# Paced gather requests and fixed-order heads in a two-layer streaming encoder

## The chip, the cores and the metric

The kernel runs on one core of one Trainium2 chip. The metric is the device time of one execution in microseconds. The core's engines are PE (matmul), DVE (vector), ACT (scalar), POOL (GpSimd, which here also issues the gathers) and SP (which issues the weight loads); each runs its own instructions in order and waits for the others by semaphores. Sixteen DMA engines move all data.

## What is computed

One inference step of a two-layer encoder for 384 tokens of width 1024: one prompt of 256 frames and eight streams of 16 further frames. Layer 0 mixes with a Mamba-2 scan, layer 1 with sliding-window attention; each is followed by a PEER layer, in which every token picks 128 of 16384 experts by product keys:

```python
def peer(xn, w_q, sub_k1, sub_k2, u_tab, v_tab):
...
        q = (xb @ w_q).reshape(PEER_TOKEN_BLOCK, PEER_HEADS, PEER_QDIM)
        s1 = jnp.einsum('thd,nd->thn', q[..., :PEER_HALF], sub_k1)
        s2 = jnp.einsum('thd,nd->thn', q[..., PEER_HALF:], sub_k2)
        v1, i1 = lax.top_k(s1, PEER_TOPK)
        v2, i2 = lax.top_k(s2, PEER_TOPK)
...
        gate = jax.nn.softmax(vs.astype(jnp.float32), axis=-1).reshape(PEER_TOKEN_BLOCK, PEER_HEADS * PEER_TOPK)
        ue = jnp.take(u_tab, eid, axis=0)
        act = jax.nn.gelu(jnp.einsum('tkd,td->tk', ue, xb).astype(jnp.float32))
        ve = jnp.take(v_tab, eid, axis=0)
        return jnp.einsum('tk,tkd->td', (gate * act).astype(xb.dtype), ve)
...
            h = h + mix
            h = h + peer(rmsnorm(h, norm_ffn[l]), p_w_q[l], p_sub_k1[l], p_sub_k2[l], p_u[l], p_v[l])
        y = rmsnorm(h, norm_final)
```

## The kernel before

The 384 tokens are three blocks of 128: blocks 0 and 1 are the prompt (256 tokens), block 2 holds the streams. h lies in SBUF as [128, 3, 1024]. Matmuls in full precision are made of three passes: `split` cuts a tile into hi (ACT, L130 or L133) and lo (DVE, L131 or L134), and `gemm_cols` and `gemm_rows` multiply hi·hi, hi·lo and lo·hi.

The program runs in one line: Mamba mixer (to 384 us of the profiled span), `peer(0)` (to about 1320), the shared key and value projection and attention (to about 1475), `peer(1)` (to 2412), `final`.

A PEER layer treats its two groups of tokens differently. For the **prompt** it multiplies with all experts: pass 1 has 128 steps, one for each row of 128 experts, of u products (L166 to L168), pass 2 has 128 steps of v products (L179). I number the steps 0 to 127 and 128 to 255. From step 64 on the order of PE, DVE and ACT is held to the order in which the code is written (`in_order`); POOL and SP are ordered by a scheduler, which places an instruction by its readiness in a simulated execution. For the **streams** (block 2) it gathers only the rows that are picked, 128 x 1024 floats (512 KB) per gather, all issued by POOL in one queue (L1232):
- a *u row* (`fetch_u`) goes into one of three or four buffers `gath`, and DVE multiplies it with the tokens (L1279, `u_item`). `U_DUE` says how many are done by which step, and each is asked for two or three items ahead.
- four *v rows* make a *quad* (`fetch_v`, `v_quad`): sixteen matmuls with the coefficients `cm` (L1349). `V_DUE` says at which step a quad stands. A row needs a *place*, four slots of the big array G, from the list `V_SLOTS`, and `taken` notes which are in use; a place is free again as soon as its quad is written.
- an *item* (`fetch_item`, `v_item`) is a v row that DVE adds up itself (L1304), from step `I_DUE[0]` on.

`tick` and `quads` are called once per step and write these requests down.

At the head of `peer` each block of h gets the mixer's result (`add`: L653 in layer 0, L919 in layer 1), is squared on ACT (L971), its mean goes to the power −1/2 on POOL (L976), it is scaled on DVE (L979) and transposed on PE (L988), and the query products follow. The tile qTp takes both the squares' output and the scaled rows. h then goes to DRAM (`spill`) and comes back near the end of pass 2 (L1591), where the PEER result is added (L1597). The attention head and `final` repeat that norm through `rstd_of` (L200 to L204) and `normed_T` (L223, L227).

Of the kernel before, what the change touches and what calls it, by code (L numbers as in the profile page):

```python
# [19 lines left out]
P = 128  # L20
# [46 lines left out]
def encoder_step(ctx: ExitStack, tc: tile.TileContext, t_in, t_out):  # L67
# [102 lines left out]
    def gemm_rows(accs, terms, first, last):  # L170


        for b, halves in enumerate(accs):
            n = halves[0].shape[-1]
            for i, ((whi, wlo), xhi, xlo) in enumerate(terms):
                st, sp = first and i == 0, last and i == len(terms) - 1
                for x, w, s_, e_ in ((xhi(b), whi, st, False), (xhi(b), wlo, False, False), (xlo(b), whi, False, sp)):
                    for hf, ps in enumerate(halves):
                        mm = pe.matmul(ps, x, w[:, hf * n:(hf + 1) * n], start=s_, stop=e_)  # L179
                        if len(terms) > 1:  # L180
                            pin(mm)
# [10 lines left out]
    def rstd_of(h, order=range(NB)):  # L192

        ss = T(small, [P, NB], F32, tag="ss")
        s2 = T(small, [P, NB, 2], F32, tag="ss2")
        r = T(small, [P, NB], F32, tag="rstd")
        for b in order:
            c = slice(b, b + 1)
            for hf in range(2):
                sq = act.activation(bank([P, 512]), h[:, b, hf * 512:hf * 512 + 512], AF.Square,  # L200
                                    accum_out=s2[:, b, hf:hf + 1])
            dve.tensor_tensor(ss[:, c], s2[:, b, 0:1], s2[:, b, 1:2], op=OP.add)
            dve.tensor_scalar(ss[:, c], ss[:, c], 1.0 / D, EPS, op0=OP.mult, op1=OP.add)
            pool.tensor_tensor(r[:, c], ss[:, c], mhalf[:, c], op=OP.pow)  # L204
        after["act"] = sq
        return r

    after = {}

    @contextmanager  # L210
    def behind():

        with ExitStack() as c:
            for i in after.values():
                c.enter_context(tc.issue_after(i.ins))
            yield

    def normed_T(pls, xn, h, r, gis, use, order):

        outs = [(T(pl, [P, KD, NT], F32R, tag=f"xhi{i}"), T(pl, [P, KD, NT], F32R, tag=f"xlo{i}"))  # L220
                for i, pl in enumerate(pls)]
        for b in order:
            after["dve"] = dve.tensor_scalar(xn[:, b], h[:, b], r[:, b:b + 1], None, op0=OP.mult)  # L223
        for k in range(KD):
            ps = bank([P, NT])
            for b in order:
                pe.transpose(ps[:, b * P:(b + 1) * P], xn[:, b, k * P:(k + 1) * P], ident)  # L227
            for (hi, lo), gi in zip(outs, gis):
                split(hi[:, k], lo[:, k], ps, scale=gcol[:, gi, k:k + 1])
            use(k, outs)  # L230
        return outs
# [18 lines left out]
    def mamba(h_src):  # L250
        with ExitStack() as c:
# [17 lines left out]
            with tc.tile_pool(name="mxn", bufs=1) as xn_pool:  # L269
                xn = T(xn_pool, [P, NB, D], F32, tag="xn")  # L270
                r = rstd_of(h)
                for b in range(NB):
                    dve.tensor_scalar(xn[:, b], h[:, b], r[:, b:b + 1], None, op0=OP.mult)
# [48 lines left out]
            if True:  # L322
# [327 lines left out]
                def add(b):  # L650
# [7 lines left out]
    def attention():  # L658
        with ExitStack() as c:
# [41 lines left out]
            for s in range(NSEQ):  # L701
                pool.memset(maskS[:, s, P + s * TS:P + (s + 1) * TS], 0.0)
# [1008 lines left out]
```

## Time and profile before

| | us |
|---|---|
| median of 3 runs | 2423.77 (2420.09 to 2424.36) |
| the profiled execution | 2425.08 |
| its span | 2423.4 |
| PE busy | 2321.5 |
| DVE busy | 1964.2 |
| ACT busy | 1250.2 |
| POOL busy | 768.1 |

The profile shows one execution. A row of the timeline has the start and length in us, the engine, the line of the kernel, the operation, what it writes and reads, how many, and in brackets how long the engine stood idle before it and what released it. The queue `q1` carries the loads of SP and `q0` those of POOL; here are their packets, their bytes, and the time of their packets as a share of the span of all sixteen DMA engines:

```profile
q1 hardware_dynamic: 99936, 365.85, 41.7%
q0 software_dynamic: 76928, 281.07, 31.1%
```

Most of q0 is gathers: 256 u rows, 192 v rows and 64 items for the two layers, 512 KB each.

### The profile page before, as it was taken

What the parts mean: (1) busy time and instruction counts of PE and PEld (TensorE: products, weight loads), DVE (VectorE), ACT (ScalarE), POOL (GpSimd) and SP (SyncE); (2) the same over time, 40 slices, a digit from 0 to 9 for tenths busy, and PEclk for the clock granted to TensorE, in tenths of its full rate; (3) what the DMA queues carried; (4) which work ended last, traced back from release to release, by engine and by line L of the source; (5) the groups of instructions that cost most, each with busy time, mean ns of one, the idle gap of its engine ahead of it and who ended that gap; (6) DMA issues with size and microseconds to landing.
All of it is one profiled execution on the core that took longest, in us unless ns stands there. A gap on an engine that the chain in (4) does not pass through costs nothing.

```text
span 2423.4 us, 44427 instructions
## 1 busy us (share of the span) xinstructions
PE 2321.5 (96%) x16591; PEld 1991.9 (82%) x16592; DVE 1964.2 (81%) x4233; ACT 1250.2 (52%) x2428; POOL 768.1 (32%) x779
## 2 busy tenths in 40 slices
PE   8899999999998999999998998999998999998997
PEld 7899988999997997666776777999997897666675
DVE  5988846979987899887776675979987899887776
ACT  5656524434565676563343554344475666554343
POOL 2222200011244334555562100012244434556561
PEclk9999999999999999999999999999999999999999
DMA  5555434457798889999995415366798889999995
GB/s 203 175 187 179 154 136 160 137 203 243 261 334 309 319 310 328 399 389 388 369 417 169 149 62 171 123 219 238 257 333 313 307 307 332 399 392 378 384 407 187
DMA packets 177080, 649.76 MB, mean 268 GB/s; under 512 B 21136, under 2 KB 23040, under 8 KB 174208
## 3 DMA queue, kind: packets, MB, share of 16 engines
q1 hardware_dynamic: 99936, 365.85, 41.7%
q0 software_dynamic: 76928, 281.07, 31.1%
q8 instruction: 130, 2.13, 0.4%
q14 instruction: 86, 0.70, 0.1%
HBM read 630.62 MB, written 18.06 MB: 268 GB/s over the span
## 4 chain that ended last, share of the span: by engine, by line
PE 79%; DVE 9%; DMA 4%; issue 3%; ACT 2%; another core or an unknown queue 1%; POOL 1%; SPq 0%; POOLq 0%; DVEq 0%; ACTq 0%
PE bank L179 26%; PE bank L166 11%; PE bank L168 11%; PE bank L167 11%; PE bank L1349 4%; PE bank L1437 3%; DVE lo L131 3%; DMA gath<-in_p_u,eidU 3%; PE bank L1404 2%; PE bank L1362 2%; ACT hi L130 1%; DVE gath L1279 1%; PE bank L533 1%; PE bank L472 1%
## 5 line engine op out<-in xcount | busy, mean ns | idle before, releaser
L130 ACT CAST hi<-raw 128x1024 fp32r<-128x1024 f32 (+1 forms) x476 | 495.8, 1042 | 686.5 <-PE bank L167 318.8
L131 DVE TENSOR_TENSOR lo<-raw,hi 128x1024 fp32r<-128x1024 f32 (+1 forms) x476 | 576.4, 1211 | 172.1 <-ACT hi L130 153.5
L1232 POOL DMA_INDIRECT gath<-in_p_u,eidU x226 | 279.7, 1238 | 779.3 <-DVE gath L1279 443.0
L168 PE MATMUL bank<-xhi,lo 128*128 128x256 f32 (+1 forms) x1344 | 397.0, 295 | 24.1 <-DVE lo L131 22.8
L166 PE MATMUL bank<-xhi,hi 128*128 128x256 f32 (+1 forms) x1344 | 403.5, 300 | 0.5 <-issue 0.4
L167 PE MATMUL bank<-xlo,hi 128*128 128x256 f32 (+1 forms) x1344 | 393.9, 293 | 0.0
L1232 POOL DMA_INDIRECT G<-in_p_v,eidT x192 | 236.7, 1233 | 155.6 <-PE bank L1349 98.4
L168 PEld LDWEIGHTS bank<-xhi,lo 128*128 128x128 f32 x1344 | 255.3, 190 | 29.5 <-DVE lo L131 27.3
L166 PEld LDWEIGHTS bank<-xhi,hi 128*128 128x128 f32 x1344 | 255.7, 190 | 15.6 <-issue 7.8
L167 PEld LDWEIGHTS bank<-xlo,hi 128*128 128x128 f32 x1344 | 255.6, 190 | 0.5
L166 PE MATMUL bank<-qhi,hi 128*128 128x256 f32 (+1 forms) x784 | 232.8, 297 | 0.0
L168 PE MATMUL bank<-qhi,lo 128*128 128x256 f32 (+1 forms) x784 | 227.5, 290 | 2.4 <-DVE lo L131 2.4
L167 PE MATMUL bank<-qlo,hi 128*128 128x256 f32 (+1 forms) x784 | 228.4, 291 | 0.0
L130 ACT CAST hix<-raw 128x1024 fp32r<-128x1024 f32 x118 | 123.9, 1050 | 194.7 <-PE bank L179 85.5
L179 PE MATMUL bank<-hi,phi 128*128 128x512 f32 x632 | 204.3, 404 | 0.2
L1392 ACT ACTIVATE oa<-ioh,e2T 128x128 f16<-128x128 f16 x512 | 163.4, 390 | 79.7 <-PE bank L1404 67.2
L179 PE MATMUL bank<-lo,phi 128*128 128x512 f32 x632 | 197.0, 393 | 6.8 <-DVE lo L131 6.8
L179 PE MATMUL bank<-hi,plo 128*128 128x512 f32 x632 | 195.5, 391 | 0.0
L131 DVE TENSOR_TENSOR lox<-raw,hix 128x1024 fp32r<-128x1024 f32 x118 | 143.9, 1219 | 29.3 <-ACT hix L130 25.1
L1279 DVE SCALAR_TENSOR_TENSOR gath<-gath,G 128x1024 f32<-128x1024 f32 x112 | 136.4, 1219 | 37.2 <-DMA gath<-in_p_u,eidU 37.2
L168 PEld LDWEIGHTS bank<-qhi,lo 128*128 128x128 f32 x784 | 148.1, 189 | 2.8 <-DVE lo L131 2.8
L167 PEld LDWEIGHTS bank<-qlo,hi 128*128 128x128 f32 x784 | 148.8, 190 | 0.4
(396 smaller groups left out, 5155.0 us busy)
## 6 DMA issues: line engine op xcount, KB each, us to landing
raw<-in_u_t SPq DMA_DIRECT2D x256, 512.0 KB
raw<-in_p_v SPq DMA_DIRECT2D x256, 512.0 KB
raw<-in_w_in SPq DMA_DIRECT2D x32, 512.0 KB
raw<-in_p_w_q SPq DMA_DIRECT2D x32, 512.0 KB
raw<-in_w_z SPq DMA_DIRECT2D x16, 512.0 KB
s<-in_state_ssm SPq DMA_DIRECT2D x8, 1024.0 KB
out_sm_ssm<-s SPq DMA_DIRECT2D x8, 1024.0 KB
raw<-in_w_out SPq DMA_DIRECT2D x16, 512.0 KB
```

The source lines that it names most:

```text
L130: act.copy(hi, raw)
L131: dve.tensor_tensor(lo, raw, hi32, op=OP.subtract)
L166: pe.matmul(ps, whi[:, s], xhi[:, k, c0:c1], start=(k == 0), stop=False)
L167: pe.matmul(ps, whi[:, s], xlo[:, k, c0:c1], start=False, stop=False)
L168: pe.matmul(ps, wlo[:, s], xhi[:, k, c0:c1], start=False, stop=(k == KD - 1))
L179: mm = pe.matmul(ps, x, w[:, hf * n:(hf + 1) * n], start=s_, stop=e_)
L1232: pool.indirect_dma_start(out=tile_, out_offset=None, in_=tab, in_offset=bass.IndirectOffsetOnAxis(ap=idx, axis=0))
L1279: pin(dve.scalar_tensor_tensor(tile_, tile_, 1.0, xg[g], op0=OP.mult, op1=OP.mult, accum_out=au[g][:, j:j + 1]))
L1349: pe.matmul(out_s[hf][32 * q:32 * q + 32, :], cm[:, q], rows[q][:, hf * 512:hf * 512 + 512], start=(r == 0), stop=False, tile_position=(0, ...
L1362: pe.matmul(ps, wt[0][:, k * P:(k + 1) * P], xf[:, k], start=(k == 0), stop=(k == KD - 1))
L1392: act.activation(a[:, i], ioh, AF.Square, scale=-1.0, bias=e2T[:, t, 0:1])
L1437: pe.matmul(accs[b][hf], G[e2 // HE][:, e2 % HE, b * P:(b + 1) * P], wt[0][:, hf * 512:hf * 512 + 512], start=False, stop=False)
```

## The change

Requests: `room` grows by `PACE`, 1.6, with each step, up to 1.6; every gather takes one off, and a v row or an item is only asked for while `room` is not negative. A place counts as free two steps after its quad. `V_DUE`, `V_SLOTS`, `U_DUE` and `I_DUE` have new numbers.

Heads: the class `Norm` takes the place of `rstd_of`; the mean is one DVE instruction, the factor 1/1024 goes into the square. At the head of `peer`, at the end of pass 2, at the head of attention and in `final` the adds, squares, powers and scales of the three blocks stand interleaved in a fixed order; qTp and sk move into a pool of their own at lower addresses; the masks of attention are written after the norms' powers; the transposes at the attention head are written several times over. `gemm_rows` runs its last call one half of a bank after the other. The spill is three DMAs.

```diff
-I_DUE = (203, 250)
+I_DUE = (206, 250)
+PACE = 1.6
-U_DUE = ((64, 22), (128, 68), (192, 115), (203, P))
-V_DUE = ([82, 86, 90, 94, 98, 103] + [149 + 6 * i for i in range(10)] + [207 + 11 * (i // 2) for i in range(8)])
-V_SLOTS = [(1, 36 + 4 * i, 66, 100 + 4 * i) for i in range(6)] + [(0, e, 128 + e + 5, 256) for e in (0, 4, 8, 12, 20, 24, 28, 32)]
+U_DUE = ((64, 22), (128, 68), (192, 115), (206, P))
+V_DUE = [82, 85, 90, 95, 102, 148, 156, 162, 167, 171, 177, 181, 186, 192, 197, 203,
+         213, 218, 223, 228, 233, 237, 243, 247]
+V_SLOTS = [(1, e, 66, 64 + e) for e in range(28, 60, 4)] + [(0, e, 128 + e + 5, 256) for e in (0, 4, 8, 12, 20, 24, 28, 32, 56, 60)] + [(0, 16, 209, 256)]
...
+            m = len(halves)
+            for part in ([[hf] for hf in range(m)] if last else [range(m)]):
+                for i, ((whi, wlo), xhi, xlo) in enumerate(terms):
...
+                        for hf in part:
+                            mm = pe.matmul(halves[hf], x, w[:, hf * n:(hf + 1) * n], start=s_, stop=e_)
...
+    class Norm:
...
+        def rstd(self, b):
             c = slice(b, b + 1)
+            dve.scalar_tensor_tensor(self.ss[:, c], self.s2[:, b, 0:1], EPS, self.s2[:, b, 1:2], op0=OP.add, op1=OP.add)
+            self.last = pool.tensor_tensor(self.r[:, c], self.ss[:, c], mhalf[:, c], op=OP.pow)
...
+            with in_order():
+                nrm.scale(2, xn[:, 2])
+                nrm.rstd(0)
+                ends(1, 0)
...
+                ends(1, 1)
+                nrm.scale(0, xn[:, 0])
+                nrm.rstd(1)
...
+                nrm.scale(1, xn[:, 1], 2)
+                for b, n in ((2, 3), (0, 2), (1, 1)):
+                    for _ in range(n):
+                        turn(range(5), [b])
...
+            with tc.issue_after(nrm.last.ins):
+                masked()
+                constants()
...
+            qp0 = tc.tile_pool(name="pq0", bufs=1)
...
+            qTp = T(qpool0, [P, 2 * PH, NP], F32, tag="qTp")
...
-                for b in range(NB):
-                    add(b)
-                    squares(b)
-                    normed(b, 1 + (b == 2))
...
+                sums(0, 0)
+                sums(0, 1)
+                sums(1, 0)
+                nrm.rstd(0)
+                nrm.scale(0, xn[0])
+                sums(1, 1)
+                sums(2, 0)
+                nrm.rstd(1)
+                sums(2, 1)
+                nrm.scale(1, xn[1])
+                nrm.rstd(2)
+                nrm.scale(2, xn[2], 2)
...
-                taken.add(slot)
+                taken[slot] = 2 * NKEY + HE
+                room[0] -= 1
...
-                    taken.discard(slot)
+                    taken[slot] = s + 2
...
+            def ends(b, hf):
+                hh = h[:, b, hf * 512:hf * 512 + 512]
+                dve.tensor_tensor(hh, hh, (accs[b] if b < 2 else out_s)[hf], op=OP.add)
+                nrm.square(b, hf)
...
+                room[0] = min(room[0] + PACE, PACE)
...
-                if s % 4 == 3 and s < V_DUE[0]:
-                    return
-                if done["f"] < (first if s < 2 * HE else 4 * len(QR)) and v_slot(done["f"], s):
+                if (done["f"] < (first if s < 2 * HE else 4 * len(QR)) and room[0] >= 0 and v_slot(done["f"], s)):
...
+                if e2 == 2 * HE - 2:
+                    ends(2, 0)
+                    ends(2, 1)
+                    nrm.rstd(2)
+            ends(0, 0)
+            ends(0, 1)
...
+                out(2, 0, D)
+                nrm.rstd(0)
+                ends(1, 0)
+                ends(1, 1)
+                out(0, 0, 512)
+                nrm.rstd(1)
+                out(0, 512, D)
+                out(1, 0, 512)
+                out(1, 512, D)
```

Three places show how the instructions move. First POOL in pass 2 of layer 0, where the last u rows are gathered (`gath` and `gathx` are u rows; `G<-in_p_v,eidT` are v rows and `G<-in_p_v,eidU` items; x4 is four such rows in turn). Before:

```order
L1232 DMA G_626_3975<-in_p_v,eidT_3971 128x1024 x4
L1232 DMA gath_13237<-in_p_u,eidU_3964 128x1024
L1232 DMA gathx_13263<-in_p_u,eidU_3964 128x1024
L1232 DMA gath_13289<-in_p_u,eidU_3964 128x1024
L1232 DMA gath_13314<-in_p_u,eidU_3964 128x1024
L1232 DMA gath_13341<-in_p_u,eidU_3964 128x1024
L1232 DMA gathx_13375<-in_p_u,eidU_3964 128x1024
L1232 DMA G_626_3975<-in_p_v,eidT_3971 128x1024 x3
```

and now:

```order
L1250 DMA G_626_3972<-in_p_v,eidT_3968 128x1024 x4
L1250 DMA gath_13083<-in_p_u,eidU_3961 128x1024
L1250 DMA gathx_13149<-in_p_u,eidU_3961 128x1024
L1250 DMA gath_13175<-in_p_u,eidU_3961 128x1024
L1250 DMA gath_13203<-in_p_u,eidU_3961 128x1024
L1250 DMA G_626_3972<-in_p_v,eidT_3968 128x1024 x3
L1250 DMA gath_13259<-in_p_u,eidU_3961 128x1024
L1250 DMA G_626_3972<-in_p_v,eidT_3968 128x1024
```

Six u rows between two quads have become four; the four v rows of a quad still stand together.

Second, DVE at the end of pass 2 of layer 0, where h (`h_14759`, now `h_14762`) gets its sums: the first two of these rows write block 2 and wait for h from DRAM; lo and plo belong to the last v tiles. Before:

```order
L1597 TENSOR_TENSOR h_14759<-h_14759,bank_7480 128x512
L1597 TENSOR_TENSOR h_14759<-h_14759,bank_7481 128x512
L131 TENSOR_TENSOR lo_14765<-raw_14762,hi_14764 128x1024
L131 TENSOR_TENSOR plo_14769<-G_1210_7475,phi_14768 128x256
L202 TENSOR_TENSOR ss_14920<-ss_2551_14921 128x1
L203 TENSOR_SCALAR ss_14920<-ss_14920 128x1
L131 TENSOR_TENSOR lo_14787<-raw_14784,hi_14786 128x1024
```

and now:

```order
L133 TENSOR_TENSOR lo_14815<-raw_14812,hi_14814 128x1024
L133 TENSOR_TENSOR plo_14819<-G_1210_7478,phi_14818 128x256
L133 TENSOR_TENSOR lo_14837<-raw_14834,hi_14836 128x1024
L133 TENSOR_TENSOR plo_14841<-G_1210_7478,phi_14840 128x256
L1468 TENSOR_TENSOR h_14762<-h_14762,bank_7483 128x512
L1468 TENSOR_TENSOR h_14762<-h_14762,bank_7484 128x512
L210 SCALAR_TENSOR_TENSOR ss_14765<-ss_2511_14766 128x1
```

The sums of block 2 have moved behind the last lo.

Third, ACT at the head of `peer(1)`, with what the rows wait for: casts of the last weight tile of attention and of the first one of the queries, and between them the six squares into qTp. Before:

```order
L130 CAST hi_16463<-raw_16461 128x1024 [waits DMAHW3_49,DVE_49,PE_49]
L130 CAST hix_16543<-raw_16536 128x1024 [waits DMAHW4_49]
L971 ACTIVATE qTp_16531,ss_2856_16541<-h_14759 128x512 [waits DVE_49,PE_49]
L971 ACTIVATE qTp_16531,ss_2856_16541<-h_14759 128x512 [waits DVE_49] x5
L1021 CAST hi_16603<-raw_16538 128x1024 [waits DMAHW5_49,Activation_49]
```

and now:

```order
L132 CAST hi_16485<-raw_16483 128x1024 [waits DMAHW6_49,DVE_49,PE_49]
L132 CAST hix_16571<-raw_16563 128x1024 [waits DMAHW7_49]
L205 ACTIVATE qTp_16554,ss_2856_16568<-h_14762 128x512 [waits DMASW4_49,DMASW3_49,DMASW5_49,DMASW2_49,DMASW6_49,DMASW1_49,DMASW7_49,DMASW0_49,DVE_49]
L205 ACTIVATE qTp_16554,ss_2856_16568<-h_14762 128x512 [waits DVE_49] x5
L1038 CAST hi_16632<-raw_16565 128x1024 [waits DMAHW0_49,PE_49,Activation_49]
```

The first square waits for transfers of POOL's queue and DVE where it waited for PE.

More of the change, by code (lines that the diff above doesn't have):

```diff
@@ L174, in gemm_rows @@
             n = halves[0].shape[-1]
[L175 to L181, printed above, removed]
+            m = len(halves)
+            for part in ([[hf] for hf in range(m)] if last else [range(m)]):
+                for i, ((whi, wlo), xhi, xlo) in enumerate(terms):
+                    st, sp = first and i == 0, last and i == len(terms) - 1
+                    for x, w, s_, e_ in ((xhi(b), whi, st, False), (xhi(b), wlo, False, False), (xlo(b), whi, False, sp)):
+                        for hf in part:
+                            mm = pe.matmul(halves[hf], x, w[:, hf * n:(hf + 1) * n], start=s_, stop=e_)
+                            if len(terms) > 1:
+                                pin(mm)
     def gemm_row_loop(accs, terms):
@@ L190, in gemm_row_loop @@
                 held, n = [], n + 1
[L192 to L197, printed above, removed]
-            c = slice(b, b + 1)
[L199 to L231, printed above, removed]
+    class Norm:
+        def __init__(self, h):
+            self.h = h
+            self.ss = T(small, [P, NB], F32, tag="ss")
+            self.s2 = T(small, [P, NB, 2], F32, tag="ss2")
+            self.r = T(small, [P, NB], F32, tag="rstd")
+        def square(self, b, hf, out=None):
+            act.activation(bank([P, 512]) if out is None else out, self.h[:, b, hf * 512:hf * 512 + 512], AF.Square,
+                           scale=1.0 / 32, accum_out=self.s2[:, b, hf:hf + 1])
+        def rstd(self, b):
+            c = slice(b, b + 1)
+            dve.scalar_tensor_tensor(self.ss[:, c], self.s2[:, b, 0:1], EPS, self.s2[:, b, 1:2], op0=OP.add, op1=OP.add)
+            self.last = pool.tensor_tensor(self.r[:, c], self.ss[:, c], mhalf[:, c], op=OP.pow)
+        def scale(self, b, out, parts=1):
+            for i in range(parts):
+                w = slice(i * D // parts, (i + 1) * D // parts)
+                dve.tensor_scalar(out[:, w], self.h[:, b, w], self.r[:, b:b + 1], None, op0=OP.mult)
@@ L270, in mamba @@
                 xn = T(xn_pool, [P, NB, D], F32, tag="xn")
-                r = rstd_of(h)
+                nrm = Norm(h)
                 for b in range(NB):
-                    dve.tensor_scalar(xn[:, b], h[:, b], r[:, b:b + 1], None, op0=OP.mult)
+                    nrm.square(b, 0)
+                    nrm.square(b, 1)
+                    nrm.rstd(b)
+                for b in range(NB):
+                    nrm.scale(b, xn[:, b])
                 split(wdh, wdl, wdt)
@@ L728, in attention, with turn @@
-            (khi, klo), (qhi, qlo) = normed_T((kpool, xpool), xn, h, r, (4, 1), kv_block, DONE)
+            ends, nrm = hold.pop("end")
+            khi, klo = [T(kpool, [P, KD, NT], F32R, tag="xhi0"), T(kpool, [P, KD, NT], F32R, tag="xlo0")]
+            qhi, qlo = [T(xpool, [P, KD, NT], F32R, tag="xhi1"), T(xpool, [P, KD, NT], F32R, tag="xlo1")]
+            kw = {0: load_raw(t_in["w_kv"][0:P, :], 512)}
+            turned = {}
+            def turn(ks, bs):
+                for k in ks:
+                    if k not in turned:
+                        turned[k] = bank([P, NT])
+                    for b in bs:
+                        pe.transpose(turned[k][:, b * P:(b + 1) * P], xn[:, b, k * P:(k + 1) * P], ident)
@@ L963, in peer, with sums @@
             raws = [load_raw(t_in["p_w_q"][l, ct]) for ct in range(2)]
[L964 to L979 removed]
+            nrm = Norm(h)
+            def sums(b, hf):
+                add(b, hf)
+                nrm.square(b, hf, xn[b][:, hf * 512:hf * 512 + 512])
             turned = {}
@@ L1251, in v_slot @@
             def v_slot(n, s):
-                return next((k for *k, s0, s1 in V_SLOTS if s0 <= s and V_DUE[n // 4] <= s1 and tuple(k) not in taken), None)
-            taken = set()
+                return next((k for *k, s0, s1 in V_SLOTS if s0 <= s and V_DUE[n // 4] <= s1 and taken.get(tuple(k), 0) <= s), None)
+            taken = {}
+            room = [0.0]
             due = []
@@ L1460, in tick @@
                     fetch_u(done["u"] + 2 + ("u" in more))
+                    room[0] -= 1
                     u_item(done["u"])
```

134 lines of the change are left out of this document (64 added, 70 removed).

## The prediction, written before the changed kernel had run

> **What bounds the kernel now.** I read the page's busy table first, then windows of the stages and of 20 us, then the chain of work that ended last and the timeline of each engine at the places where PE, the TensorE matmul engine, stands still.
>
> ```profile
> PE 2321.5 (96%) x16591; PEld 1991.9 (82%) x16592; DVE 1964.2 (81%) x4233; ACT 1250.2 (52%) x2428; POOL 768.1 (32%) x779
> ```
>
> PE is busy 2321.5 of 2423.4 us, so a microsecond is gained only where PE is idle or runs at a lower clock. The change takes no matmul away (it adds 31 transposes), so some 102 us are to be shared out. The windows say where the gaps of the two passes lie (columns: window, then for PE, PEld, DVE, ACT, POOL the busy us, then the granted clock, the DMA share and GB/s).
>
> ```profile
> 655.00:893.00 238.00, 227.72 (x2260) 213.57 (x2259) 203.63 (x313) 152.96 (x310) 95.65 (x82) 0.99 0.88 317
> 893.00:1297.00 404.00, 396.20 (x2207) 284.31 (x2205) 337.66 (x522) 204.22 (x377) 205.79 (x164) 0.99 0.96 371
> 740.00:760.00 20.00, 14.65 (x115) 12.84 (x116) 12.44 (x21) 8.47 (x18) 6.57 (x7) 0.88 0.87 322
> 1080.00:1100.00 20.00, 20.00 (x129) 13.60 (x129) 17.87 (x31) 10.41 (x21) 11.58 (x9) 1.00 0.99 390
> 1120.00:1140.00 20.00, 15.20 (x64) 9.85 (x63) 13.29 (x22) 5.30 (x8) 9.87 (x8) 0.83 0.93 351
> ```
>
> The first row is the second half of pass 1 of layer 0, the second its pass 2: PE idles 10.3 and 7.8 us there, and a mean clock of 0.99 costs 1% more, 2.4 and 4 us, so about 12 us can be won in each of the four passes. In 740–760 PE loses 5.4 us, in 1120–1140 4.8 us, and the clock falls as well. In 1080–1100, with the DMA engines just as full (0.99, 390 GB/s), PE loses nothing. So a full DMA alone does not stop PE. The same pairs of dips come again in layer 1, some 1092 us later.
>
> All terms below are against the profiled execution, 2425.08 us (span 2423.4 and 1.7 around it). The median of the runs shown is 2423.77, 1.3 lower; I take that off at the end.
>
> **The change, part by part: requests in pass 2.** What stops PE near 1124 us:
>
> ```profile
> 1107.48 1.74 POOL L1232 DMA_INDIRECT G<-in_p_v,eidT  x1 [1.56 <-PE bank L1349]
> 1113.68 1.55 POOL L1232 DMA_INDIRECT gath<-in_p_u,eidU  x1 [0.30 <-issue]
> 1119.30 0.94 POOL L1232 DMA_INDIRECT gath<-in_p_u,eidU  x1 [0.30 <-issue]
> 1113.68 11.94 DMA gath<-in_p_u,eidU
> 1125.65 1.23 DVE L1279 SCALAR_TENSOR_TENSOR gath<-gath,G 128x1024 f32<-128x1024 f32 x1 [7.13 <-DMA gath<-in_p_u,eidU]
> 1128.61 3.64 PE L1349 MATMUL bank<-G,cm 128*32 128x512 f32 x16 [4.80 <-DVE cm L1336]
> ```
>
> POOL waits for the quad's matmuls (L1349) to release the places, then sends four v rows back to back from 1107.48 on and four u rows behind them. The u row sent at 1113.68 takes 11.94 us to land; DVE stands 7.13 us on it, the quad's coefficients (cm) stand behind that product in DVE's fixed order, and PE waits 4.80 us. Three or four u rows are in flight at once. Between steps 192 and 203 the old table asks for 13 u rows in 11 steps; at some 3.2 us a step that is one in 2.7 us, and three in flight cover 8 us, less than 11.94. The new table asks for 13 in 14 steps, one in 3.4 us, so three cover 10 and four 13.6 us. Counted by the planner's rules, all requests there fall from 9 in four steps to 6.
>
> But the order of POOL's instructions shows that the four v rows still stand together and are followed by four u rows, since they still wait for the same matmuls of PE. So the wait shrinks and does not go: I take **a little under half of the 12, −5.5 us per layer, −11 for both**. Ends: 0, and −12 per layer.
>
> **Requests in pass 1.** The two stalls of layer 0:
>
> ```profile
> 730.05 0.96 POOL L1232 DMA_INDIRECT G<-in_p_v,eidT  x1 [0.72 <-PE bank L1349]
> 748.12 0.94 POOL L1232 DMA_INDIRECT G<-in_p_v,eidT  x1 [6.90 <-PE bank L1349]
> 756.09 0.69 DVE L1410 SCALAR_TENSOR_TENSOR G<-bank,G 128x512 f32<-128x512 f32 x1 [6.70 <-remote]
> 757.97 0.38 PE L168 MATMUL bank<-xhi,lo 128*128 128x256 f32 x1 [3.54 <-DVE lo L131]
> ```
>
> Each time POOL has just waited for a quad (0.72 and 6.90 us) and issues five or six gathers in 7 us; DVE then waits 6.70 us for an answer from PE, and PE 3.54 us for the lo that stands behind. After the change POOL's order has eight v rows at the start instead of six, then again three u rows, four v rows, two u rows and four v rows (before: three and one around a u row). The stretch that stalls is the same; only what follows is thinner. I take **−1 us per layer, −2**; ends +3 per layer (the longer first burst, and the second quad due one step sooner, priced at the 3.54) and −12.
>
> **Heads and tails.** Head of peer(0), first three DVE rows, then PE:
>
> ```profile
> 382.53 1.40 DVE L653 SCALAR_TENSOR_TENSOR h<-bank,rs,h 128x512 f32<-128x512 f32 x2
> 386.21 1.41 DVE L653 SCALAR_TENSOR_TENSOR h<-bank,rs,h 128x512 f32<-128x512 f32 x2
> 389.21 0.88 DVE L979 TENSOR_SCALAR qTp<-h,rstd 128x512 f32<-128x512 f32 x2 [0.65 <-POOL rstd L976]
> 386.44 1.28 PE L988 MATMUL bank<-ident,qTp 128*128 128x128 f32 x10 [1.80 <-DVE qTp L979]
> 389.76 1.50 PE L988 MATMUL bank<-ident,qTp 128*128 128x128 f32 x6 [2.03 <-DVE qTp L979]
> 390.00:393.00 3.00, 3.00 (x13) 2.87 (x13) 1.24 (x3) 1.57 (x4) 0.00 (x0) 0.50 0.62 262
> ```
>
> Block after block, DVE adds two halves (1.41), waits for ACT's squares and POOL's power, and scales: 3.68 us from add to add. In the new order the adds of the next block fill those waits. DVE's own work is six halves (4.2), three scales (2.4) and three sums (0.5), 7.1 us where 11.3 were taken; but the last block's add, squares, power and scale stay one behind the other. PE's waits here are 1.80 and 2.03 us. I take **−2** (ends 0 and −5.5: both waits, and 1.7 for the stretch at a clock of 0.50).
>
> Head of peer(1), ACT, then DVE, then PE:
>
> ```profile
> 1475.04 0.63 ACT L971 ACTIVATE qTp<-h 128x512 f32<-128x512 f32 x1 [7.04 <-PE bank L179]
> 1469.36 1.28 DVE L919 TENSOR_TENSOR h<-h,bank 128x512 f32<-128x512 f32 x2
> 1484.39 0.88 DVE L979 TENSOR_SCALAR qTp<-h,rstd 128x512 f32<-128x512 f32 x2 [0.65 <-POOL rstd L976]
> 1478.15 0.41 PE L988 MATMUL bank<-ident,qTp 128*128 128x128 f32 x2 [3.15 <-DVE qTp L979]
> 1481.72 2.37 PE L988 MATMUL bank<-ident,qTp 128*128 128x128 f32 x10 [3.16 <-DVE qTp L979]
> 1479.00:1486.00 7.00, 3.44 (x15) 3.07 (x16) 3.34 (x8) 4.74 (x12) 1.09 (x2) 0.50 0.37 158
> ```
>
> The first square writes into qTp, which lies on the place of attention tiles that the last matmuls read; so it waits 7.04 us, until 1475.04, though block 0 is added from 1469.36 on. With qTp in a pool of its own it waits only for output DMAs sent long before. Blocks 0 and 1 are then finished behind PE's matmuls. Block 2 is left: add, squares, sum, power, scale, 0.64+0.80+0.16+0.66+0.88 = 3.1 us behind PE's end at 1475.0, so 1478.2 instead of 1485.27. Some of these 7 us is spent on the transposes of three blocks at 0.12 to 0.25 us each: **−6** (ends −2, and −12: PE's idle of 3.15 and 3.16 and 0.8 more at the next wait, and the time lost at a clock of 0.50).
>
> End of peer(0) and head of attention:
>
> ```profile
> 1304.77 1.28 DVE L1597 TENSOR_TENSOR h<-h,bank 128x512 f32<-128x512 f32 x2 [6.21 <-PE bank L179]
> 1307.24 0.72 PE L179 MATMUL bank<-lo,phi 128*128 128x512 f32 x2 [2.06 <-DVE lo L131]
> 1324.52 0.33 PE L227 MATMUL bank<-ident,oT 128*128 128x128 f32 x1 [3.92 <-DVE oT L223]
> 1308.00:1312.00 4.00, 4.00 (x12) 3.12 (x11) 1.35 (x2) 0.81 (x2) 1.45 (x1) 0.57 0.46 131
> 1325.00:1332.00 7.00, 5.56 (x20) 4.61 (x20) 3.26 (x6) 2.53 (x5) 4.41 (x7) 0.51 0.75 166
> 1331.57 0.17 DVE L715 TENSOR_SCALAR nsnk<-snk 128x16 f32<-128x16 f32 x1 [2.79 <-DMA snk<-in_sinks]
> ```
>
> The sum for block 2 stands ahead of the last lo tiles and waits for h coming back from DRAM (6.21 us of DVE idle); PE waits 2.06 us. It now stands behind the last lo. The masks that POOL writes ahead of the norms' powers go behind them, and repeated transposes fill PE's wait of 3.92. On the other side, where gemm_rows runs half a bank at a time, the last tile's lo is needed after four matmuls, not eight, so that lo is waited for about 0.9 us longer; and the sink loads, which DVE waited 2.79 us for at 1331.57, are issued no sooner, so this wait remains. In 1325–1332 the clock is 0.51: 5.56 us of PE work in it would be some 2.8 at full clock. Sum 2.0 + 3 + 1 − 0.9: **−5** (ends +1 and −12).
>
> The Trainium skill ("TensorE: Matmul & The Clock Gate", What's actually happening) says that an idle window of about 3.4 us halves the rate and that as long a busy one restores it. The trace agrees on the length, and halves already after a gap of 2.06 us (0.57 in 1308–1312). By that rule the repeated transposes would keep the clock up, and this term would be −8.
>
> The end of the program:
>
> ```profile
> 2398.61 1.28 DVE L1597 TENSOR_TENSOR h<-h,bank 128x512 f32<-128x512 f32 x2 [6.03 <-DMA h<-hd]
> 2401.09 0.73 PE L179 MATMUL bank<-lo,phi 128*128 128x512 f32 x2 [1.88 <-DVE lo L131]
> 2412.11 0.61 PE L179 MATMUL bank<-hi,plo 128*128 128x512 f32 x2
> 2415.07 2.48 DVE L1606 SCALAR_TENSOR_TENSOR y<-h,rstd,g 128x1024 f32<-128x1024 f32 x2 [1.25 <-DMA g<-in_norm_final]
> 2418.46 1.28 DVE L1606 SCALAR_TENSOR_TENSOR y<-h,rstd,g 128x1024 f32<-128x1024 f32 x1 [0.66 <-POOL rstd L204]
> ```
>
> The same sum blocks PE for 1.88 us. At the end, y of blocks 2 and 0 (2.48 us, behind a wait of 1.25 for g) stands ahead of block 1's sum and power. Behind PE's last matmul at 2412.72 there were 7.0 us to the last y at 2419.74. Now: add 0.65, square 0.8, sum 0.16, half a y 0.65 over the power, two halves 1.3: 3.6 us. With 1.9 − 0.9 at the lo: **−4** (ends −1 and −6). I put the spill in three DMAs and the weight tile drawn ahead at nothing: both run under the query products that follow, and if that cover were gone, 1.5 MB at the 390 GB/s above would show as 4 us.
>
> **Sum:** −11 − 2 − 2 − 6 − 5 − 4 = −30; 2425.1 − 30 = 2395.1; less 1.3 for the median: **2394 us**.
>
> **The rivals.**
> 1. *POOL's bursts rule, the pacing changes nothing for PE.* For it: the unchanged groups of four. Against: 9 requests become 6 where PE stalls. Both passes at 0: 2407 us. Chance 0.18.
> 2. *The pacing does all it can:* fewer requests at once, so no burst delays a u row. For it: 1080–1100 shows a full DMA without a stall. Pass 2 at −9 and pass 1 at −8 each: 2394 − 7 − 14 = 2373 us. Chance 0.17. The Trainium skill ("DMA: Bandwidth & Descriptors", Measured) fits one gather's time as 2.0 us plus its bytes over 436 GB/s, an estimate of 3.2 us; the trace has 11.94, and by the rule nothing would ever be late, as in this rival.
> 3. *New waits eat the heads:* the lo of the last tile at four places, the sink loads, a DVE order that now couples three blocks. Heads at −8 instead of −17: 2403 us. Chance 0.12.
> 4. *Slower: v rows come late.* Before, a quad's last row was asked for 7 to 9 steps ahead in the middle of pass 2; now 3 steps for all, 9.6 us at 3.2 us a step. If rows take longer than that, as the 11.94 above, PE stands at L1349 itself, 2.3 us for each of some 14 quads per layer: +64, less what DVE's lead absorbs, say half, and no gain in the passes: 2407 + 32 = 2439 us. Against is the group of these matmuls in pass 2 of layer 0:
>
> ```profile
> L1349 PE MATMUL bank<-G,cm 128*32 128x512 f32 x288 | 35.7, 623 | 6.7 <-DVE cm L1336 6.7
> ```
>
> PE never waited for a row there, only for cm, although up to step 162 the lead was three to five steps before too. Chance 0.05.
>
> **How the numbers follow.** The forecast has 0.48. The range, 2370 to 2412, takes in the forecast with its ends, rivals 1 and 3 and most of 2; 0.17 is left out. About 0.2%, 5 us, is what a measurement can tell here: faster by more than that 0.90 (all but rival 4 and the worst of 1 and 3 together), same 0.05, slower 0.05.
>
> **What would show it.** Right: PE's gaps near 1124 and 2218 us under 2.5 us each; the stalls near 740 and 754 still there; ACT's first square of peer(1) waiting for DVE, not PE; the last y within 4 us of the last matmul. Wrong: PE idle before L1349 released by a DMA in many quads; a long wait of DVE for h or for the sinks ahead of the kv products; gaps in pass 1 gone, which would say that the number of gathers, and not their grouping, was the cause.

## The result and the profile after

The changed kernel took 2389.01 us in the median of four runs (2385.20 to 2391.18); the kernel before took 2424.07 (2420.09 to 2426.76, four runs). The ratio is 0.986, with a 95% interval of 0.9841 to 0.9879. Forecast were 2394 us, with a range of 2370 to 2412. Ratios leave out runs more than 1.5% longer than the fastest of the same kernel; there is one such run, in experiment 7.

The page's busy table of the changed kernel, then three windows: the second half of pass 1 of layer 0, its pass 2, and the place of the gap in pass 2.

```profile
PE 2317.2 (97%) x16607; PEld 1984.0 (83%) x16607; DVE 1964.6 (82%) x4227; ACT 1252.3 (52%) x2428; POOL 772.6 (32%) x779
664.00:884.00 220.00, 211.18 (x2147) 200.37 (x2147) 191.50 (x293) 143.41 (x292) 85.88 (x74) 0.98 0.87 315
884.00:1287.00 403.00, 400.48 (x2242) 286.37 (x2241) 343.35 (x529) 208.87 (x385) 214.06 (x170) 1.00 0.98 380
1125.00:1145.00 20.00, 17.56 (x85) 13.11 (x84) 15.27 (x24) 8.14 (x12) 12.92 (x10) 1.00 1.03 419
```

PE is busy 4.3 us less than before; the other 31.6 of the 35.9 us by which the span shrank were idle time of PE. In pass 2 the idle of PE fell from 7.8 to 2.5 us. In pass 1 it is still 8.8 (10.3 before, in a window longer by 18 us), and the mean granted clock is lower (0.98, 0.99 before).

The starts of the same matmuls in both timelines divide the span into stages, in us:

| stage, cut at | before | after | difference | forecast |
|---|---|---|---|---|
| to the first query matmul of peer(0) | 390.90 | 390.69 | −0.2 | −2 |
| to step 64, from where xhi is used | 273.05 | 273.46 | +0.4 | 0 |
| to the first v matmul (pass 1, steps 64 to 127) | 224.88 | 219.91 | −5.0 | −1 |
| to the last item's matmuls (pass 2) | 408.30 | 403.19 | −5.1 | −5.5 |
| to the first output matmul of attention | 128.29 | 120.50 | −7.8 | −5 |
| to the first query matmul of peer(1) | 60.70 | 54.41 | −6.3 | −6 |
| to step 64 | 270.68 | 270.22 | −0.5 | 0 |
| to the first v matmul (pass 1, steps 64 to 127) | 226.06 | 220.13 | −5.9 | −1 |
| to the last item's matmuls (pass 2) | 408.31 | 406.51 | −1.8 | −5.5 |
| to the end | 32.21 | 28.54 | −3.7 | −4 |

So half of the 36 us lies in the heads, tails and queries (18.0), half in the passes (17.8). The first stage holds the whole mixer, and its −0.2 says little of the head at its end, as the rows of the heads below show.

Pass 1 lost its two old stalls and has a new one. POOL, then the chain of waits, then DVE and PE:

```profile
669.00 1.99 POOL L1250 DMA_INDIRECT G<-in_p_v,eidT  x1 [0.30 <-issue]
680.00 0.94 POOL L1250 DMA_INDIRECT G<-in_p_v,eidT  x1 [0.30 <-issue]
681.24 1.85 POOL L1250 DMA_INDIRECT gath<-in_p_u,eidU  x1 [0.30 <-issue]
681.24 10.85 DMA gath<-in_p_u,eidU
692.12 1.23 DVE L1299 SCALAR_TENSOR_TENSOR gath<-gath,xg 128x1024 f32<-128x1024 f32 x1 [5.56 <-DMA gath<-in_p_u,eidU]
694.54 0.58 PE L170 MATMUL bank<-xhi,lo 128*128 128x256 f32 x1 [5.74 <-DVE lo L133]
```

Between 669.00 and 680.00 POOL sends eight v rows in one go. The u row behind them takes 10.85 us to land, DVE stands 5.56 us on it, and the lo behind that product comes 5.74 us late for PE; layer 1 has the same gap (5.88 us). It is the mechanism that I had found in pass 2, at a place where before there were six rows.

In pass 2 the mechanism of before is still there, but smaller: chain, DVE, PE, the group of the quads' matmuls in this stage, and the wait at the same place of layer 1.

```profile
1129.21 9.92 DMA gathx<-in_p_u,eidU
1139.16 1.23 DVE L1299 SCALAR_TENSOR_TENSOR gathx<-gathx,G 128x1024 f32<-128x1024 f32 x1 [3.21 <-DMA gathx<-in_p_u,eidU]
1142.12 1.92 PE L1370 MATMUL bank<-G,cm 128*32 128x512 f32 x16 [2.44 <-DVE cm L1357]
L1370 PE MATMUL bank<-G,cm 128*32 128x512 f32 x304 | 36.6, 598 | 2.4 <-DVE cm L1357 2.4
2212.23 3.45 PE L1370 MATMUL bank<-G,cm 128*32 128x512 f32 x16 [4.12 <-DVE cm L1357]
```

The u row takes 9.92 us where it took 11.94, PE waits 2.44 us where it waited 4.80. Over the whole stage the quads wait 2.4 us for cm (6.7 before), and for no v row. In layer 1 the wait is 4.12 us, 5.69 before.

The heads: in peer(0) the mixer's first output matmul and the first query matmul, before and then after, with DVE and PE between them in the changed kernel; then ACT, DVE and PE in peer(1); then the end of pass 2 and the attention head (PE, PE, DVE); then the last matmul and the last y.

```profile
307.22 0.71 PE L179 MATMUL bank<-hi,yhi 128*128 128x512 f32 x2
390.90 0.67 PE L1027 MATMUL bank<-qhi,hix 128*128 128x384 f32 x1
308.64 0.71 PE L183 MATMUL bank<-hi,yhi 128*128 128x512 f32 x2
382.72 0.75 DVE L641 SCALAR_TENSOR_TENSOR h<-bank,rs,h 128x512 f32<-128x512 f32 x1 [0.62 <-PE bank L183]
386.80 0.75 DVE L641 SCALAR_TENSOR_TENSOR h<-bank,rs,h 128x512 f32<-128x512 f32 x1 [0.24 <-PE bank L183]
386.37 0.39 PE L183 MATMUL bank<-hi,ylo 128*128 128x512 f32 x1
390.69 0.45 PE L1044 MATMUL bank<-qhi,hix 128*128 128x384 f32 x1
1452.44 0.64 ACT L205 ACTIVATE qTp<-h 128x512 f32<-128x512 f32 x1 [2.08 <-DVE h L939]
1460.60 0.88 DVE L216 TENSOR_SCALAR qTp<-h,rstd 128x512 f32<-128x512 f32 x2 [0.65 <-POOL rstd L211]
1460.02 0.85 PE L999 MATMUL bank<-ident,qTp 128*128 128x128 f32 x6 [1.08 <-DVE ss L210]
1302.72 0.49 PE L183 MATMUL bank<-lo,phi 128*128 128x512 f32 x1 [0.45 <-DVE lo L133]
1311.66 1.07 PE L714 MATMUL bank<-ident,oT 128*128 128x128 f32 x5 [1.11 <-DVE oT L216]
1320.21 0.17 DVE L763 TENSOR_SCALAR nsnk<-snk 128x16 f32<-128x16 f32 x1 [1.06 <-DMA snk<-in_sinks]
2378.99 0.39 PE L183 MATMUL bank<-hi,plo 128*128 128x512 f32 x1
2382.69 1.41 DVE L1637 SCALAR_TENSOR_TENSOR y<-h,rstd,g 128x512 f32<-128x512 f32 x2 [0.44 <-POOL rstd L211]
```

In peer(1) the first square now waits 2.08 us for DVE's sum instead of 7.04 for PE, and the last scale ends 3.2 us behind PE's last matmul. In peer(0) the mixer's last matmul ends at 386.76, where before it ended near 384.4. But the mixer starts its output matmuls at a different time in each profile: 307.22 us in this profile of the kernel before and 309.74 in the second one (run 5), 308.64 and 308.03 in those of the changed kernel (run 6 is the second). From that start to the first query matmul it takes 83.68 and 83.73 us before, 82.05 and 82.05 after; so the end of the mixer and the head together gained 1.7 us. Of it the mixer's output matmuls lost 0.9 (77.20 us before, 78.12 after, 77.21 in run 12, which leaves out the order by halves), and behind the mixer's last matmul 2.6 us are won (6.48 before, 3.93 after). At the last lo of pass 2 PE waits 0.45 us behind 0.76 for phi. The sinks cost DVE 1.06 us (and 0.54 for the second load) instead of 2.79 (and 1.24). The last y ends 4.7 us behind the last matmul instead of 7.0.

### The profile page after: what moved, and what is told of

Read it like the earlier page. It is cut to its first block, busy times and chain, and to the rows that moved or that the text cites. A ratio compares the mean times of both kernels' runs of the same rounds, so it can differ in the third digit from the quotient of the medians.

```text
span 2387.5 us, 44460 instructions
## 1 busy us (share of the span) xinstructions
PE 2317.2 (97%) x16607; PEld 1984.0 (83%) x16607; DVE 1964.6 (82%) x4227; ACT 1252.3 (52%) x2428; POOL 772.6 (32%) x779
## 4 chain that ended last, share of the span: by engine, by line
PE 82%; DVE 6%; DMA 4%; issue 3%; ACT 2%; POOL 2%; another core or an unknown queue 0%; SPq 0%; POOLq 0%; DVEq 0%; ACTq 0%
PE bank L183 27%; PE bank L168 12%; PE bank L170 12%; PE bank L169 11%; PE bank L1370 3%; PE bank L1458 3%; PE bank L1383 2%; PE bank L1425 2%; DVE lo L133 2%; DMA gath<-in_p_u,eidU 1%; POOL G L1250 1%; DMA gathx<-in_p_u,eidU 1%; ACT hi L132 1%; DMA ab<-acum_rows 1%; PE bank L522 1%
## 5 line engine op out<-in xcount | busy, mean ns | idle before, releaser
L1250 POOL DMA_INDIRECT gath<-in_p_u,eidU x226 | 292.8, 1296 | 787.6 <-DVE gath L1299 455.3
L1250 POOL DMA_INDIRECT G<-in_p_v,eidT x192 | 232.6, 1212 | 138.6 <-PE bank L1370 80.6
L1299 DVE SCALAR_TENSOR_TENSOR gath<-gath,xg 128x1024 f32<-128x1024 f32 x114 | 138.7, 1217 | 16.5 <-DMA gath<-in_p_u,eidU 16.5
L183 PEld LDWEIGHTS bank<-hi,phi 128*128 128x128 f32 x632 | 113.9, 188 | 45.6 <-ACT phi L132 14.1
```

Source lines behind the costliest of these rows:

```text
L183: mm = pe.matmul(halves[hf], x, w[:, hf * n:(hf + 1) * n], start=s_, stop=e_)
L1250: pool.indirect_dma_start(out=tile_, out_offset=None, in_=tab, in_offset=bass.IndirectOffsetOnAxis(ap=idx, axis=0))
L1299: pin(dve.scalar_tensor_tensor(tile_, tile_, 1.0, xg[g], op0=OP.mult, op1=OP.mult, accum_out=au[g][:, j:j + 1]))
```

## The experiments

The kernel before was timed again beside each group of four runs, and the three groups ran on three chips. Its median differed from group to group: 2424.07 with the changed kernel, 2410.20 beside the first four runs, 2420.40 beside the next four, 2423.36 beside the last four. The changed kernel differed less: 2389.01, 2389.33 (run 3, which is the changed kernel in all but name) and 2388.41. So times of different groups are compared below only with care.

**1. Requests alone.** The kernel before with the tables, the count `room` and the late places of the change.

```diff
-I_DUE = (203, 250)
+I_DUE = (206, 250)
+PACE = 1.6
...
-                    taken.discard(slot)
+                    taken[slot] = s + 2
```

> The kernel before with the requests of the change alone (its tables, the count per step, places free two steps late); heads, norms and gemm_rows as before. If the two halves of the change simply add up, the two passes give back what the traces show there (5.0 and 5.9 us in pass 1, 5.1 and 1.8 in pass 2 of the two layers, 18 in all): about 2406 us, with the gaps of PE near 740 and 754 us gone and a new one near 689 us. If instead the passes gained because the new heads bring DVE into them earlier, this gives little: 2415 us or more.

Measured: 2403.76 us, ratio 0.9969 (0.9955 to 0.9984) to a kernel before that stood at 2410.20. The time is the one expected, the gain is a third of it: the stretch near 689 us has the worst gap of the layer.

```profile
696.24 0.58 PE L170 MATMUL bank<-xhi,lo 128*128 128x256 f32 x1 [7.63 <-DVE lo L133]
```

**2. Heads alone.** The changed kernel with the requests of before.

```diff
-I_DUE = (206, 250)
-PACE = 1.6
+I_DUE = (203, 250)
...
-                    taken[slot] = s + 2
+                    taken[slot] = 0
```

> The changed kernel with the requests of before (tables, no count per step, a place free at once). If the halves add up: about 2406 us, with the gaps near 740 and 754 us back and the head of peer(1) still 7 us shorter. If the new heads need the new requests: above 2412.

Measured: 2395.68 us, ratio 0.9941 (0.9925 to 0.9958). With 2410.20 beside them, the heads are worth 14.5 us and the requests 6.4, and both together (run 3) 20.9: the halves add up. In the other groups the whole change is worth 32 to 35 us; how the further 11 to 14 us divide was not measured. The head of peer(1) is 3.87 us long from the last output matmul to the first query matmul, as in the changed kernel (11.12 before). But the gaps near 740 and 754 us did not come back. The old requests stall near 689 us too:

```profile
691.63 0.58 PE L168 MATMUL bank<-xhi,lo 128*128 128x256 f32 x1 [5.14 <-DVE lo L131]
```

In pass 2 the two profiles do separate the halves. The wait at the last u rows is short with the new requests (run 1), long with the old ones (run 2), whatever the heads:

```profile
1140.48 3.07 PE L1354 MATMUL bank<-G,cm 128*32 128x512 f32 x16 [1.95 <-DVE cm L1341]
1122.06 3.64 PE L1366 MATMUL bank<-G,cm 128*32 128x512 f32 x16 [5.08 <-DVE cm L1353]
```

**3. The count lifted.**

```diff
-PACE = 1.6
+PACE = 1000.0
```

> The changed kernel with the count per step lifted (1000 a step in place of 1.6), tables and late places kept. If the tables and the late places carry the gain, since POOL's order hardly changes: within 3 us of the changed kernel, 2386 to 2392. If the count of 1.6 does it: the gaps of PE at the last u rows of pass 2 grow back and it is 5 to 9 us slower, 2394 to 2398.

Measured: 2389.33 us, ratio 0.9914 (0.9892 to 0.9936). The 1.6 requests per step, after which the change is named, do nothing that can be measured.

**4. POOL's order held.** The changed kernel; the gathers are kept in the order in which they are written.

```diff
-                pool.indirect_dma_start(out=tile_, out_offset=None, in_=tab,
-                                        in_offset=bass.IndirectOffsetOnAxis(ap=idx, axis=0))
+                pin(pool.indirect_dma_start(out=tile_, out_offset=None, in_=tab,
+                                            in_offset=bass.IndirectOffsetOnAxis(ap=idx, axis=0)))
```

> The changed kernel with POOL's gathers held to the order in which they are written, so that v rows and u rows really alternate. If the gap of 5.7 us near 689 us (1757 in layer 1) comes from the eight v rows sent in one go ahead of u rows, it goes, with the half clock behind it: 8 to 14 us faster than the changed kernel, 2375 to 2381. Rival: rows that could go now wait behind u rows whose buffer DVE still holds, v rows come late and PE waits at the quads' matmuls: 2392 or more.

Measured: **2362.28 us**, ratio 0.9803 (0.9787 to 0.9819), 27 us below run 3 of the same group and ahead of both kernels. The gain is twice the expected. POOL at the start of the quads, then the two passes of layer 0:

```profile
676.70 1.33 POOL L1250 DMA_INDIRECT gath<-in_p_u,eidU  x1 [0.30 <-issue]
678.34 1.09 POOL L1250 DMA_INDIRECT G<-in_p_v,eidT  x1 [0.30 <-issue]
681.17 0.93 POOL L1250 DMA_INDIRECT gath<-in_p_u,eidU  x1 [1.74 <-DVE gath L1299]
664.00:873.00 209.00, 206.40 (x2143) 196.42 (x2142) 190.96 (x292) 143.32 (x292) 85.47 (x74) 1.00 0.90 331
873.00:1274.00 401.00, 400.91 (x2248) 286.76 (x2248) 344.80 (x529) 208.47 (x385) 207.64 (x170) 1.00 0.98 382
```

u rows (`gath`) and v rows (`G`) alternate, POOL waits for DVE between them, and within the passes no u row has more than two v rows directly ahead of it (up to eight in the changed kernel). Pass 1 takes 209.4 us, 219.9 in the first profile of the changed kernel, and pass 2 400.7 instead of 403.2, with PE idle for 0.1 us of it.

**5 and 6. Both kernels again**, side by side, without an edit.

> The kernel before, unchanged, profiled beside the runs that follow. It is to show where the stalls of pass 1 lie on this chip: near 740 and 754 us as in the first profile, if they belong to the program alone; near 688 us as in the run with the old requests and new heads, if the six v rows sent in one go there stall PE on some chips and not on others.

> The changed kernel, unchanged, on the chip of the runs beside it, as the base for them: within 4 us of the run without the count per step on the earlier chip (2389) if chips differ mainly in the kernel before; a gap near 689 us of 5.7 to 7.1 us in both layers.

Measured: 2420.18 us for the kernel before (one run), 2388.41 for the changed one, ratio 0.9857 (0.983 to 0.9884). The stalls of pass 1 move. The kernel before now waits here:

```profile
741.31 0.39 PE L168 MATMUL bank<-xhi,lo 128*128 128x256 f32 x1 [1.23 <-DVE lo L131]
757.61 0.39 PE L168 MATMUL bank<-xhi,lo 128*128 128x256 f32 x1 [0.60 <-DVE lo L131]
```

1.23 us where it was 1.97, 0.60 where it was 3.54, and two waits of 1.50 and 2.45 us at 780 and 785 are new. In the changed kernel the longest wait near 689 us is 1.46 us here, 5.74 in its first profile. The stage to the first v matmul took 221.84 and 219.75 us in the two layers before, 216.29 and 216.71 after: −5.6 and −3.0. So a single gap in pass 1 is not a property of the program. The stage became shorter in both pairs and both layers, but by 3.0 to 5.9 us, and the same kernel's stages differ by 3 to 6 us between its two profiles.

**7. The kernel before with POOL's order held**, the edit of run 4.

> The kernel before with one edit: POOL's gathers held to the order in which they are written. If the grouping on POOL is what cost the passes, this alone gives most of what the pinned changed kernel gave over the changed one (27 us): 20 to 35 us faster than before. If holding the order needs places that come free late (here a v row asked for in the step of its quad stops the whole queue until PE is done), it gives little or loses: within 5 us of before, with POOL waiting for PE ahead of many v rows.

Measured: 2440.50 us in the median of ten runs, which spread from 2418 to 2457; ratio 1.0069 (1.0036 to 1.0103): slower, by some 17 us. Held order alone is not the remedy. PE's worst wait in pass 2 of layer 0, for coefficients that are made when the last u product of a group is done:

```profile
1149.70 1.26 PE L1261 MATMUL bank<-ident,cm 128*128 128x32 f32 x8 [4.34 <-DVE cm L1286]
```

**8. Order held, count lifted.** The edits of runs 3 and 4 together.

> The changed kernel with the gathers held to their order and the count per step lifted. Held to the order the count can act: if 1.6 a step is worth something then, this is 3 to 12 us slower than the pinned changed kernel (2362), mostly in pass 2; if the tables already spread the requests, within 3 us of it.

Measured: 2362.65 us, ratio 0.9746 (0.9722 to 0.9769), against 2388.41 for the changed kernel in the same group. The count does nothing with the order held either.

**9. Order held, places free at once.**

```diff
-                    taken[slot] = s + 2
+                    taken[slot] = s
```

> The pinned changed kernel (2362 us) with one edit: a place counts as free in the step of its quad, as before, not two steps later. If the late places are what makes the held order pay, POOL now stops at v rows until PE has done the quad, u rows behind them come late, and pass 2 grows by 4 us or more per layer: 2372 to 2395. If the new tables alone do it: within 3 us of 2362.

Measured: 2390.47 us, ratio 0.9849 (0.9823 to 0.9874). Without the two steps the 28 us by which runs 4 and 8 stand lower are gone. The group of POOL's gathers of v rows says why (count, busy us, mean ns, then POOL's idle ahead of them and what ended it), for the kernel before, the changed kernel, and runs 4, 8, 7 and 9:

```profile
L1232 POOL DMA_INDIRECT G<-in_p_v,eidT x192 | 236.7, 1233 | 155.6 <-PE bank L1349 98.4 <-issue 41.8 <-PE bank L1437 5.0
L1250 POOL DMA_INDIRECT G<-in_p_v,eidT x192 | 232.6, 1212 | 138.6 <-PE bank L1370 80.6 <-issue 43.7 <-PE bank L1458 4.7
L1250 POOL DMA_INDIRECT G<-in_p_v,eidT x192 | 223.4, 1164 | 70.2 <-issue 48.5 <-PE bank L1370 14.0 <-ACT hi L132 2.5
L1250 POOL DMA_INDIRECT G<-in_p_v,eidT x192 | 230.5, 1200 | 69.7 <-issue 49.5 <-PE bank L1370 11.0 <-PE bank L183 2.8
L1232 POOL DMA_INDIRECT G<-in_p_v,eidT x192 | 232.3, 1210 | 278.8 <-PE bank L1349 229.5 <-issue 44.8 <-ACT hi L130 1.6
L1250 POOL DMA_INDIRECT G<-in_p_v,eidT x192 | 218.6, 1138 | 305.8 <-PE bank L1370 258.1 <-issue 42.2 <-PE bank L1425 1.8
```

POOL's queue stands still ahead of v rows for the quads' matmuls of PE for 98.4 us before, 80.6 in the changed kernel, but 14.0 and 11.0 with the order held and the places late, and 229.5 and 258.1 with the order held and the places free at once. Behind a gather that waits for a quad all later gathers wait. In run 9 this shows in the v rows more than in the u rows: seven times PE waits for a v row, 9.2 us in all, as rival 4 had it, each time by little. DVE's waits for u rows come to 13.9 us there, 7.8 in run 4 and 36.1 in the changed kernel. PE's idle time in the four passes is 24.2 us in run 9 and 4.7 in run 4; not all of the difference is traced to a wait.

```profile
1114.31 1.92 PE L1370 MATMUL bank<-G,cm 128*32 128x512 f32 x16 [1.62 <-DMA G<-in_p_v,eidT]
```

**10. New heads, old requests, order held.** The edits of runs 2 and 4.

> New heads, all requests as before (tables, places free at once, no count), gathers held to their order. The kernel before with held order stood at 2440, 20 above before; the heads were worth 18. If heads and requests add up: 2415 to 2425, with pass 2 of layer 1 near 426 us. If the new heads let DVE run further ahead so that the held order works with the old requests too: below 2390.

Measured: 2411.31 us, ratio 0.9954 (0.9929 to 0.998), and pass 2 of layer 1 at 416.4 us (425.7 in run 7). A little below the expected sum. Against run 2, the same heads and requests without the held order, the time is 16 us longer, but that run belongs to another group, and the ratios to the kernel before beside each (0.9954 and 0.9941) do not differ; in the profiles the four passes are 13.5 us longer than in run 2. So the old requests gain nothing from the held order with these heads either; that they lose is likely, not shown.

**11. Each transpose once** at the attention head.

```diff
-                for b, n in ((2, 3), (0, 2), (1, 1)):
+                for b, n in ((2, 1), (0, 1), (1, 1)):
```

> The changed kernel with each transpose at the attention head written once, not one to three times. By the page's rule on the clock gate, and the half clock of 1325 to 1332 us before, PE then stands still for some 4 us there, the clock halves, and the stage from the first kv matmul to the first output matmul of attention grows by 1.5 to 3.5 us from its 95 to 97. If the repeats do nothing for the clock: unchanged within 1 us, and no half clock between 1300 and 1320.

Measured: 2392.73 us in one run, no difference. Half of the expectation holds. The clock halves, but the stage does not grow (seven us around the first kv matmuls, run 11 and then the changed kernel):

```profile
1314.00:1321.00 7.00, 5.83 (x16) 4.58 (x17) 3.16 (x6) 1.97 (x4) 6.89 (x21) 0.53 0.35 90
1312.00:1319.00 7.00, 6.85 (x31) 4.94 (x30) 4.90 (x9) 4.72 (x9) 6.89 (x21) 1.00 0.46 118
```

The clock is 0.53 instead of 1.00, yet the stage from the first kv matmul to the first output matmul takes 95.00 us, 95.08 with the repeats in the first profile of the changed kernel and 97.04 in the second. A cost below 2 us would not show in that spread. That PE, slower there, catches up inside its waits for ACT and DVE is a reading, not shown.

**12. Both halves of a bank in turn**, as before.

```diff
-            for part in ([[hf] for hf in range(m)] if last else [range(m)]):
+            for part in ([range(m)]):
```

> The changed kernel with gemm_rows writing both halves of a bank in turn in its last call, as before. My 0.9 us at the last lo: the two gaps of 0.76 and 0.45 us at each end of pass 2 shrink to 0.2 and the stage from the items' end to the last v matmul falls from 20.4 to 19.5. What the halves give back: block 1's first sum starts later, so 0.5 to 0.9 us are lost again behind it (5.0 us to the first kv matmul becomes 5.6, 3.9 to the first query matmul 4.5). Net within 2 us. If the halves matter for more than that, the two stages behind the last matmul grow by over 1.5 us each.

Measured: 2390.47 us in one run, no difference. From the last item to the last v matmul it takes 19.41 us instead of 20.41, and behind it 6.00 instead of 5.01 to the first kv matmul, 4.56 instead of 3.87 to the first query matmul, 8.95 instead of 8.16 to the end. The halves cost 1.0 us ahead of the last matmul and give 0.7 to 1.0 back behind it.

## Why the prediction held, and where it did not

The sum was −30 us, and −35.8 came (profile against profile); −33.3 came between the profiles of runs 5 and 6. That the total came this near is partly luck: in the first pair pass 1 gave 8.9 us more than taken in its two layers, pass 2 gave 4.1 less. Term by term:

- **Pass 2, −5.5 per layer:** mechanism and size right on the whole, unevenly (−5.1 and −1.8; −5.1 and −2.9 between runs 5 and 6). Half of the wait went in layer 0, as taken (4.80 to 2.44 us), less in layer 1 (5.69 to 4.12, where I had asked for under 2.5). Runs 1 and 2 show that the requests did it. I missed that the new table moves one quad per layer, 1.9 us of PE work (16 matmuls, as in the row at 1142.12), from pass 1 to pass 2, so that the stage won 7.0 and 3.7 net of it, in idle time and clock together.
- **Pass 1, −1 per layer:** this step failed. I wrote that "the stretch that stalls is the same", and it was not: the gaps near 740 and 754 us went, and the longer first burst, for which I had only an upper end of +3, cost 5.74 us of PE. Net of the quad that moved, which takes 1.9 us away here, the stage won 3 to 4 us (1 to 4 with the second pair of profiles). I had read two gaps of one profile as properties of two bursts. Runs 2 and 5 show the old requests with other gaps, near 689 or 785 us.
- **Head of peer(0), −2:** right, though the stage shows −0.2. Counted from the mixer's first output matmul, the gain is 1.6 to 1.7 us in both pairs of profiles; the stage as cut also holds the mixer ahead of it, which came 1.4 us later in the first profile of the changed kernel and differs by 5 us over the profiles of all runs. The half-bank order, which costs 0.9 us at the mixer's last lo (0.46 and 0.76 us of waiting, for 0.52 before), I had counted at the other ends only; without it the head is worth 2.6 us.
- **Head of peer(1), −6:** right, −6.3 (−6.2 between runs 5 and 6), and by the step named: the square no longer waits for PE.
- **End of peer(0) and attention head, −5:** right in direction; in size −7.8, but −4.8 between runs 5 and 6, so the difference from −5 is within what profiles of one kernel differ by. That the sinks' wait would remain was half right: DVE's waits for them fell from 2.79 and 1.24 to 1.06 and 0.54 us in the first profiles, but the first is 3.38 us in run 12. The rule of the Trainium skill on the clock gate ("TensorE: Matmul & The Clock Gate", What's actually happening) gave −8, nearly the measured number of the first pair; but run 11 takes the repeats out, and the stage stays, so the agreement is chance. The repeats are 15 more transposes by the profiles (39 for 24), not the 31 that I had counted.
- **The end, −4:** right, −3.7, in its size; the last y came 4.7 us behind the last matmul, where I had written within 4, so of the 3.4 us that I took there 2.3 came, and 1.2 ahead of the last matmul.
- **The lo of the last tile, +0.9:** right, 1.0 in run 12; that the halves give it back behind the last matmul I had put inside the sums, not as their price.

Of the rivals, the first was half right: the count of 1.6 changes nothing (runs 3 and 8). It was wrong in what followed from it, because tables and places are worth 6.4 us (runs 1 to 3) without it. Of the sign that I had set for it, gaps in pass 1 gone, which was to say that the number of gathers and not their grouping is the cause, half came: two gaps went, one came behind the longest group, and run 4, with the same gathers ungrouped, has it no more. That speaks for the grouping. The second, that rows which are not grouped stall nobody, came true only in run 4, with 2362 us, outside the range on the fast side; as a forecast for this change it failed, since the change does not ungroup them. The fit of 3.2 us quoted there stands on that page of the Trainium skill under "Anatomy of one DMA — SWDGE (gpsimd) path", not under "Measured". The third did not come: the heads gained 18.0 us, of 17 forecast. The fourth shows in run 9 at a few quads.

What the change is worth in full was hidden by the scheduler: the late places belong to an order in which requests are written, and POOL's order is not that one. Shown by runs 4, 7, 8 and 9: held order without late places loses with the old requests (run 7) and gains nothing with the new tables (run 9); tables, late places and held order together gain 26 us on the changed kernel and, with the heads, 58 on the kernel before (runs 8 and 6, with 2420.40 beside them). No run holds the order with the old tables and late places, so the tables' own share in this stays open.

Open is how the gaps of pass 1 near 740 and 754 us arise. There DVE waited for "another core or an unknown queue" (`remote` in the row at 756.09), which no run explains; that they move from group to group with the kernel unchanged is all that was shown. Open with it is how much of pass 1's gain the requests made: run 2 has no gap there either, with the old requests.

## What to carry to other kernels

When requests are paced in the code, look at the order on the queue that issues them: a scheduler that goes by readiness puts together again what the code spread. Hold the order only where the places come free early enough, because then every wait in the queue stops all that stands behind it. And take a gap of one profile as one draw: compare the length of a stage over two profiles before you explain a gap by what stands beside it, and cut stages so that what varies ahead of a change lies outside.

## What was not expected of the hardware

One 512 KB gather took 10 to 12 us to land behind other gathers (11.94 us right behind four v rows, 10.85 behind eight, 9.92 behind three, in the chains above), while in run 4 the DMA engines moved as much with PE idle for 0.1 us: 382 GB/s over all of pass 2, 380 in the changed kernel. The wait came from grouping, not from the amount. PE's clock halved behind waits of 2.03 and 2.06 us (heads of peer(0) and of attention, before), but not behind 2.44 us in pass 2 of the changed kernel, where the window from 1125 to 1145 us shows 1.00. It stood at half for 7 us in run 11 at no cost that shows.
